# Hymba encoder block on one NeuronCore: the gate, scan and q/k/v stage as 64 slots in a written order

## The chip, the cores and the metric

One core of a Trainium2 chip runs the whole layer. A core has five engines with instruction queues of their own: PE (TensorE, matrix products), DVE (VectorE), ACT (ScalarE), POOL (GpSimd) and SP (SyncE, which only issues DMAs here). Each queue is executed strictly in order; an instruction that waits for a semaphore holds up all that stands behind it on its engine. ACT issues DMAs too, all the stores of the stage in question among them. The metric is the device time of one execution in microseconds (us), lower is better.

## The reference

Float32, T = 1024 tokens, D = 1024, one layer:

```python
h = rmsnorm(x, norm_mix_w)
z, xbc, dt_raw, q, k, v = split(h @ w_in)     # 1024 | 1536 | 32 | 1024 | 1024 | 1024 columns
xs, B, C = split(silu(conv5(xbc)))
# forward and backward chunked scan: 8 chunks of 128 tokens, 2 groups of 8 heads
seg    = a_cum[l] - a_cum[s]                   # per head, masked to l >= s
y_diag = (C B^T * exp(seg)) @ (xs*dt)          # inside a chunk
y_off  = (C @ state) * exp(a_cum)              # carried into a chunk
state  = decay * state + B^T @ (xs*dt*decay_to_end)
g   = (y_fwd + y_bwd + d_skip*xs) * silu(z);  y_ssm = rmsnorm per group(g)
q, k = rmsnorm per head(q), rmsnorm per head(k)
y_na = neighbourhood attention(q, k, v, rel_pos_bias)
x = x + concat(y_ssm, y_na) @ w_out
x = x + relu(rmsnorm(x) @ W1)^2 @ W2
```

Products are made in float32 accuracy from pairs of rounded operands: every factor is split into a high part (ACT, a copy that rounds) and a low part (DVE, a subtraction), and each product is three matmuls.

## The kernel before

The program runs in four stages: preparation and the xBC projection with the convolution (to about 172 us), the stage of this change (172 to 648 us), the attention with the output projection (to about 925 us), and the MLP. Tiles live in pools with a fixed number of buffers; a framework follows the data and puts in the semaphore waits, and a scheduler in it decides, from a model of costs, in which order each engine's instructions stand. The code only nudges it: `issue_after(mark)` forbids the work inside it to stand ahead of one instruction.

The stage computes 64 **pieces** `h[128 tokens] @ w[1024 x 512 columns]`: 16 for the gate z, then for each of two groups g 8 for q, 8 for k and 8 for v. A piece is 24 matmuls of 512 columns (8 steps along k, three products each, `mm3`, L181 to L183) into a PSUM bank. Its weights are four raw tiles of 128x1024, which `load_w` brings from HBM (L150) and splits into `wh` (ACT, L151) and `wl` (DVE, L152). There are two raw buffers for all stages and one more in this stage, so three here, and four pairs `wh`, `wl`.

After a piece:

- z: SiLU on ACT (L649), stored to `sz_dr` (L650).
- q and k (`normed`, `turned_split`): square on ACT (L330), sum per head on DVE (L332), the inverse root on POOL (`rq`, two instructions, L209 and L210), scaling on DVE (L334, from the same PSUM bank), four transposes on PE (L342, `ptq`), split into high on ACT (L194) and low on DVE (L195), and stored from ACT's queue: k by one DMA of 512 KB (L359), q by four of 128 KB (L352).
- v: split (L194, L195) and one store (L375).

Beside the pieces run, by `beside` and by the loop over `steps`:

- 14 **backward states** beside the first 18 pieces: an input loaded (L631), weighed on POOL (L416), split (L186, L187), one product `pS`, added on DVE (L617) and stored (L604).
- 32 **blocks** of decay differences: `seg_load` broadcasts two rows of `cum_dr` (`rb`, 512 KB, L391); POOL subtracts twice in place (L400); DVE selects by the mask in place (L406); ACT stores (L411). There are 4 buffers of `rb` beside the first pieces, and 1 in the later part.
- 16 **scan steps** (chunk c, group g): loads, `exp` of two blocks on ACT (L689), splits of `C`, the state and the weighed input (L186, L187), the product `pcb` (L705), D skip terms on DVE (L711, L715), `y` on POOL (L719), weighting by `pcb` on DVE (L721), state and carried products (`pS`, `py`), `yo` on DVE (L732) and its addition on POOL (L733), the inner product `pd` (L758), then addition of `pd` (L765), gate (L675), norm (ACT L677, POOL `ry` L209, L210), scaling and store of `y` (L679, L680).

Two PSUM banks named `tp` serve both the turned pieces and `pcb`. The attention then reads q, k and v back; a head pair's `q` is one DMA of 1 MB (L907).

Of the kernel before, what the change touches and what calls it, by code (L numbers as in the profile page):

```python
# [10 lines left out]
F32 = mybir.dt.float32  # L11
# [8 lines left out]
P = 128  # L20
# [36 lines left out]
def hymba_block(  # L57
# [35 lines left out]
    def enter_phase(ph, i, mm, extra):  # L93
        phase["ps"] = ph.enter_context(
            tc.tile_pool(name=f"ps{i}", bufs=1, space=PSUM, reuse_waits="tile")
        )
        phase["mm"] = mm
        phase["v"] = 4 - mm
        phase["w"] = [wp] * 3
        phase["r"] = [wp] * 2  # L100
        phase["n"] = 0
        if extra:
# [16 lines left out]
    q_dr = dr.tile([8, 4, HD, T], F32, name="q_dr")  # L119
# [4 lines left out]
    seg_dr = dr.tile([2, NT, P, 2, 512], F32, name="seg_dr")  # L124
    sb_dr = dr.tile([2, NT, P, 512], F32, name="sb_dr")
# [11 lines left out]
    def load_w(view, lo_eng, n=1024):  # L137
        pool = phase["w"][phase["n"] % len(phase["w"])]
        nb = phase["w"].count(pool)
        phase["n"] += 1  # L140
        rpool = phase["r"][phase["n"] % len(phase["r"])]
# [3 lines left out]
        hi = pool.tile([P, 1024], F32R, tag="wh", name="wh", bufs=nb)  # L145
        lo = pool.tile([P, 1024], F32R, tag="wl", name="wl", bufs=nb)
# [4 lines left out]
        nc.scalar.activation(hi[:, 0:n], raw[:, 0:n], AF.Copy)  # L151
        lo_eng.tensor_tensor(  # L152
            lo[:, 0:n], raw[:, 0:n], hi[:, 0:n].bitcast(F32), op=sub
        )
        return hi, lo

# [56 lines left out]
    with ExitStack() as ph:  # L213
# [98 lines left out]

        def hb(v):
# [5 lines left out]
        def qkv_proj(off, g):  # L319
            get = load_w_nat(w_in[0], 0, KD, off + 512 * g, nc.vector)  # L320
            for b in range(NT):
                pt = ps_mm("pq")
                for k in range(KD):
                    s = (slice(None), k, slice(b * P, (b + 1) * P))
                    mark = mm3(pt, hTh[s], hTl[s], *get(k), k == 0, k == KD - 1)
                yield b, pt, rcol[:, b : b + 1], mark.ins

        def normed(pt, rt):
            qn = hp.tile([P, 512], F32, tag="qn", name="qn", bufs=2)
            act = nc.scalar.activation(qn, pt, AF.Square, scale=rt)  # L330
            ss = hp.tile([P, 8], F32, tag="sq", name="sq", bufs=2)
            nc.vector.tensor_reduce(ss, h8(qn), axis=mybir.AxisListType.X, op=add)  # L332
            r = inv_rms(hp, ss, HD, 8, "rq")
            nc.vector.scalar_tensor_tensor(h8(qn), h8(pt), rt, hb(r), op0=mul, op1=mul)  # L334
            return qn, act.ins

        def turned_split(qn, w, mark):
            tp = ps_tp("ptq")
            with tc.issue_after(mark):
                for j in range(4):  # L340
                    s = slice(j * P, (j + 1) * P)
                    nc.tensor.transpose(tp[:, s], qn[:, s], ident)  # L342
            hl = hp.tile([P, 2, 512], F32R, tag="hl", name="hl", bufs=2)
            split_from_psum(hl[:, 0], hl[:, 1], tp, w)
            return hl.bitcast(F32).rearrange("f a (p t) -> f a p t", p=4)

        def store_q(g, b, qn, mark):
            hl = turned_split(qn, pcol[:, 80:81], mark)
            s = slice(b * P, (b + 1) * P)
            for j in range(2):  # L350
                for a in range(2):
                    nc.scalar.dma_start(  # L352
                        q_dr[4 * g : 4 * g + 4, 2 * j + (a ^ j), :, s].rearrange("p d t -> d p t"),
                        hl[j * HD : (j + 1) * HD, a],
                    )

        def store_k(g, b, qn, mark):
            hl = turned_split(qn, pcol[:, 81:82], mark)
            nc.scalar.dma_start(  # L359
                k_dr[g, :, :, :, b * P : (b + 1) * P].rearrange("a p f t -> f (a p) t"),  # L360
                hl.rearrange("f a p t -> f (a p) t"),
            )

        def qkv_units():
            held = None
            for g in range(2):
                for off in (OFF_Q, OFF_K, OFF_V):
                    for b, pt, rt, mark in qkv_proj(off, g):
                        if held is not None:
                            held(mark)  # L370
                            held = None
                        if off == OFF_V:
                            hl = hp.tile([P, 8, 2, HD], F32R, tag="hl", name="hl", bufs=2)
                            split_from_psum(hl[:, :, 0], hl[:, :, 1], h8(pt), rt)
                            nc.scalar.dma_start(v_dr[b, :, 8 * g : 8 * g + 8], hl.bitcast(F32))  # L375
                            act = None
                        else:
# [1097 lines left out]
```

## Time and profile before

| what | value |
|---|---|
| time, median of 3 runs | 1655.78 us (1651.81 to 1657.99) |
| the profiled execution's own time | 1659.05 us |
| its span | 1657.3 us (1.75 us of its time lie outside) |
| granted TensorE clock, mean over the span | 0.982 |
| DMA issues of the stage: q stores / block stores / k stores | 64 / 32 / 16 |

The columns of a window row are: the window, its length, then for PE, PEld (weight loads), DVE, ACT and POOL the busy time with the count of instructions in brackets, the granted TensorE clock, the share of DMA time and GB/s. A row of waits names engine, line and tile that waited, then what ended the wait, the total in us, how many there were, and the longest. A row of groups has line, engine, operation, tiles and shapes, count, busy us and the mean of one in ns, and the idle time before it with what ended it. In a timeline, an `[idle before <-releaser]` at the end of a row gives the stall ahead of it.

### The profile page before, as it was taken

Reading aid. Unit: us, or ns where it says so; the run is one execution under the profiler, and the core shown is the slowest. Engines: PE = TensorE matmul, PEld = TensorE weight load, DVE = VectorE, ACT = ScalarE, POOL = GpSimd, SP = SyncE. Lnnn points to the kernel's source line nnn. Section 1 sums busy time; section 2 is a strip of 40 time slices with the busy share of each in tenths; the row PEclk is TensorE's granted clock in tenths of the full one; section 3 lists DMA queues with packets and bytes.
Section 4 is the critical chain, followed back from the end, with each engine's and each line's share of the span. In section 5 each row is a group of like instructions: output and inputs, shape, how many; then the busy total and the mean of one; then the engine's idle time right before and its main releaser. Section 6 shows DMA issues by size and latency. Waiting matters only on the chain. (4 is left out here: it accounts for less than half of the span.)

```text
span 1657.3 us, 20925 instructions
## 1 busy us (share of the span) xinstructions
PE 1589.3 (96%) x7462; PEld 1300.0 (78%) x7462; DVE 1017.6 (61%) x1420; ACT 719.1 (43%) x1183; POOL 714.6 (43%) x520
## 2 busy tenths in 40 slices
PE   7999988998989999999998998999999989999999
PEld 6788867877867888887887776888888868888887
DVE  4777455477657773666665477434244388887863
ACT  5434322254334344566675334444444534433330
POOL 3000266467546744232353332344444555455551
PEclk9999999999999999999999998999999989999999
DMA  8113688897877669968772430453444486644332
GB/s 207 53 38 102 194 266 260 222 304 212 271 210 191 190 196 308 270 171 206 207 218 77 131 123 26 151 180 117 146 157 140 163 295 214 216 142 150 102 102 77
DMA packets 190243, 290.28 MB, mean 175 GB/s; under 512 B 15715, under 2 KB 106939, under 8 KB 190139
## 3 DMA queue, kind: packets, MB, share of 16 engines
q1 hardware_dynamic: 141547, 239.65, 47.4%
q10 hardware_dynamic: 47584, 45.62, 8.5%
q0 software_dynamic: 1008, 3.67, 0.5%
q8 instruction: 59, 0.97, 0.2%
q14 instruction: 45, 0.37, 0.1%
HBM read 197.27 MB, written 94.95 MB: 176 GB/s over the span
## 5 line engine op out<-in xcount | busy, mean ns | idle before, releaser
L187 POOL TENSOR_TENSOR wl<-wraw,wh 128x1024 fp32r<-128x1024 f32 x110 | 298.3, 2722 | 320.0 <-ACT wh L186 305.5
L186 ACT ACTIVATE wh<-wraw 128x1024 fp32r<-128x1024 f32 x110 | 115.5, 1054 | 150.1 <-PE px L804 50.7
L804 PE MATMUL px<-wh,ahl 128*128 128x512 f32 x512 | 162.4, 395 | 3.3 <-ACT ahl L186 3.3
L182 PE MATMUL pq<-wl,hTh 128*128 128x512 f32 x384 | 152.9, 399 | 6.7 <-DVE wl L152 6.7
L181 PE MATMUL pq<-wh,hTh 128*128 128x512 f32 x384 | 152.1, 401 | 7.0 <-ACT wh L151 5.3
L804 PE MATMUL px<-h,wh 128*128 128x512 f32 x496 | 156.0, 396 | 1.6 <-DVE x L1156 1.6
L183 PE MATMUL pq<-wh,hTl 128*128 128x512 f32 x384 | 152.4, 398 | 0.0
L187 DVE TENSOR_TENSOR ahl<-ar,ahl 128x1024 fp32r<-128x1024 f32 x56 | 114.7, 2055 | 23.3 <-ACT ahl L186 22.2
L186 ACT ACTIVATE ahl<-ar 128x1024 fp32r<-128x1024 f32 x56 | 58.2, 1052 | 140.0 <-PE px L804 76.4
L804 PEld LDWEIGHTS px<-wh,ahl 128*128 128x128 f32 x512 | 97.1, 190 | 25.0 <-ACT ahl L186 3.7
L804 PEld LDWEIGHTS px<-h,wh 128*128 128x128 f32 x496 | 93.2, 188 | 24.2 <-ACT h L191 1.8
L804 PE MATMUL px<-wl,ahl 128*128 128x512 f32 x256 | 100.9, 395 | 0.0
L400 POOL TENSOR_TENSOR rb<-rb,c 128x512 f32<-128x512 f32 x64 | 71.2, 1134 | 67.6 <-DMA rb<-cum_dr 57.0
L804 PE MATMUL px<-h,wl 128*128 128x512 f32 x248 | 98.1, 395 | 0.0
L182 PEld LDWEIGHTS pq<-wl,hTh 128*128 128x128 f32 x384 | 73.4, 191 | 22.9 <-DVE wl L152 8.4
L181 PEld LDWEIGHTS pq<-wh,hTh 128*128 128x128 f32 x384 | 73.2, 191 | 22.8 <-ACT wh L151 6.6
L151 ACT ACTIVATE wh<-wraw 128x1024 fp32r<-128x1024 f32 x58 | 60.6, 1057 | 66.8 <-DMA wraw<-in_w_in_dram 30.3
L191 ACT ACTIVATE pth<-ptp 128x384 fp32r<-128x384 f32 (+1 forms) x128 | 56.9, 457 | 66.0 <-PE ptp L1014 65.5
L183 PEld LDWEIGHTS pq<-wh,hTl 128*128 128x128 f32 x384 | 73.3, 191 | 15.0
L804 PE MATMUL pz<-h,wh 128*128 128x512 f32 x256 | 82.2, 402 | 0.4 <-DVE h L192 0.4
L804 PE MATMUL pz<-wh,ahl 128*128 128x512 f32 x256 | 80.5, 391 | 0.0
L181 PE MATMUL po<-wh,yh 128*128 128x512 f32 x192 | 76.5, 398 | 2.1 <-DVE x L888 1.8
(273 smaller groups left out, 4031.9 us busy)
## 6 DMA issues: line engine op xcount, KB each, us to landing
ar<-act_dr SPq DMA_DIRECT2D x56, 512.0 KB, 3.6
act_dr<-cq SPq DMA_DIRECT2D x49, 512.0 KB, 3.0
wraw<-in_w_in_dram SPq DMA_DIRECT2D x44, 512.0 KB, 4.3
rb<-cum_dr SPq DMA_DIRECT2D x32, 512.0 KB, 6.6
wraw<-in_w_mlp_in_dram SPq DMA_DIRECT2D x32, 512.0 KB, 4.7
wraw<-in_w_mlp_out_dram SPq DMA_DIRECT2D x32, 512.0 KB, 4.3
seg_dr<-rb ACTq DMA_DIRECT2D x32, 256.0 KB, 2.9
q_dr<-hl ACTq DMA_DIRECT2D x64, 128.0 KB, 3.8
```

The source lines that it names most:

```text
L151: nc.scalar.activation(hi[:, 0:n], raw[:, 0:n], AF.Copy)
L181: nc.tensor.matmul(pt, lhsT=ah, rhs=bh, start=first, stop=False)
L182: nc.tensor.matmul(pt, lhsT=ah, rhs=bl, start=False, stop=False)
L183: return nc.tensor.matmul(pt, lhsT=al, rhs=bh, start=False, stop=last)
L186: nc.scalar.activation(hl[0], src, AF.Copy)
L187: eng.tensor_tensor(hl[1], src, hl[0].bitcast(F32), op=sub)
L191: top = nc.scalar.activation(hi, src, AF.Copy)
L400: nc.gpsimd.tensor_tensor(rb[:, d], rb[:, d], c1[:, d, c, h0 : h0 + 4].unsqueeze(2).broadcast_to([P, 4, P]), op=sub,)
L804: nc.tensor.matmul(pt, lhsT=a, rhs=b, start=f, stop=l, skip_group_check=True)
```

## The change

The stage is written anew as a loop over 68 slots. `slot(k)` holds piece k and, in the order in which its lines stand, everything else that is done beside it. All instructions a slot issues, on every engine, are chained to the one before on the same engine (`in_order`), SP's and ACT's DMA issues too; so the scheduler has no choice left in slots 0 to 67. What is computed stays the same, and so does the number of PE's instructions.

- **Order of pieces**: z, z, then q, v, k for each group (before: q, k, v).
- **Delays**: piece k's square or split stands in slot k+1, its transposes in the middle of piece k+2, the split of the turned piece in slot k+3. A list `late` collects the transposes and the scan's products; they are issued in the middle of the next piece, after four of its eight k steps. A list `stores` collects the stores of a slot; they are issued on ACT's queue in the next slot, ahead of the work of that slot.
- **Scan steps** begin at the slots in `starts`, and spread over five slots; **blocks** are loaded at the slots in `seg_at`, subtracted and selected two slots later. The difference goes into a tile of its own, `seg` (3 buffers, later 2), and the second half stays in `rb` (3 buffers, later 2).
- **Weights**: a fourth raw buffer; all four raw loads of the next column set are issued in a set's second slot, two tiles are split in the middle of its last slot, one at the end of it, and the fourth ahead of the next set's first piece.
- **q** is laid out in DRAM like k: one store of 512 KB per piece, and four loads in place of one per head pair later. `seg_dr` and `sb_dr` become one DRAM tile per step. The loads and stores that build the bias table are spread over slots 24 to 51.

```diff
-        phase["r"] += [wx]
+        phase["r"] += [wx] * 2
...
-    q_dr = dr.tile([8, 4, HD, T], F32, name="q_dr")
+    q_dr = dr.tile([2, 2, 4, P, T], F32, name="q_dr")
...
+        cols += [off + 512 * g for g in range(2) for off in (OFF_Q, OFF_V, OFF_K)]
...
+        def piece(k):
+            j, b = divmod(k, 8)
+            pt = out_pt[k] = ps_mm("pz" if j < 2 else "pq")
+            for i in range(KD):
+                if i == 4:
+                    while late:
+                        late.pop(0)()
+                hi, lo = tiles[j][i // 2]
...
+                mm3(pt, hTh[s], hTl[s], hi[:, w], lo[:, w], i == 0, i == KD - 1)
...
+        def seg_select(n):
+            g, c, q = seg_of(n)
+            rb, seg = rbs.pop(n)
+            nc.vector.copy_predicated(
+                seg, lmask.unsqueeze(1).broadcast_to([P, 4, P]), rb[:, 1]
+            )
+            stores.append(
+                partial(nc.scalar.dma_start, seg_dr[c, g][:, q], seg.rearrange("p h s -> p (h s)"))
+            )
...
+        starts = (20, 22, 25, 27, 30, 32, 35, 38, 40, 42, 44, 47, 50, 52, 55, 57)
...
+        def slot(k):
+            j, b = divmod(k, 8)
+            if k < 64:
+                if b == 0 and j:
+                    w_splits(j, 1)
+                piece(k)
+            else:
+                while late:
+                    late.pop(0)()
+
+            if b == 1 and j < 7:
+                raw_loads(j + 1)
...
+            for f in [stores.pop(0) for _ in range(len(stores))]:
+                f()
...
+            leave(k - 1)
+            split_turned(k - 3)
+            for a in at(k, 5):
+                put_y(*a)
+            for a in at(k, 4):
+                gate(*a)
+            for a in at(k, 2):
+                diagonal(*a)
...
+            scale(k - 1)
+            for a in at(k, 4):
+                norm(*a)
+            if b == 7 and j < 7:
+                w_splits(j + 1, 2)
+            for a in at(k, 2):
+                decayed(*a)
+            if seg is not None:
+                seg_subtract(seg)
...
+            if seg is not None:
+                seg_select(seg)
+
+            for a in at(k, 0):
+                late.append(partial(products, *a))
...
+            if b == 7 and j < 7:
+                w_splits(j + 1, 1)
...
+            with in_order():
+                slot(k)
...
-            nc.sync.dma_start(q.bitcast(F32), q_dr[p].rearrange("(h a) d t -> (a d) h t", h=2))
+            for j in range(2):
+                for a in range(2):
+                    nc.sync.dma_start(
+                        q[a * HD : (a + 1) * HD, j].bitcast(F32),
+                        q_dr[p // 4, a ^ j, p % 4, j * HD : (j + 1) * HD],
+                    )
```

In the changed kernel's own lines the square is L590, the sum L592, the scaling L598, the transposes L604, the split L201 and L202, the subtraction L651, the selection L662, all stores of a slot L854 and the matmuls of a piece L188 to L190.

Where it moves instructions, at three places.

**ACT, the store of a block.** Before, in the second half of the stage (`hl` is a split piece, `wh` a weight tile, `chl`, `shl` and `xhl` operands of the scan):

```order
L680 DMA y_dr<-y_3132 128x512
L194 ACTIVATE hl<-ptq,pcol 128x512
L151 ACTIVATE wh<-wraw 128x1024
L411 DMA seg_dr<-rb 128x512
L359 DMA k_dr<-hl 128x8x128
L186 ACTIVATE chl<-cT 128x128
L186 ACTIVATE shl<-st 128x512
L194 ACTIVATE hl<-ptq,pcol 128x512
```

and in the changed kernel, two slots of the first k set:

```order
L854 DMA k_dr<-hl 128x8x128
L854 DMA seg_dr_82<-seg 128x512
L590 ACTIVATE qn<-pq,rcol 128x512
L201 ACTIVATE hl<-ptq,pcol 128x512
L825 ACTIVATE y_3461<-y_3461,ry 128x512
L826 DMA y_dr<-y_3461 128x512
L854 DMA k_dr<-hl 128x8x128
L590 ACTIVATE qn<-pq,rcol 128x512
```

The stores of the slot before, the block's among them, now stand directly ahead of the square of the last piece; before, a square stood wherever the scheduler had put it, here not next to the block's store at all.

**DVE, one slot's list.** Before, in the second group's part of the stage (`sq` the sum per head, `qn` the scaled piece, `rb` the block selected):

```order
L195 SCALAR_TENSOR_TENSOR hl<-pq,rcol,hl 128x8x64
L406 COPY_PREDICATED rb<-lmask,rb 128x512
L187 TENSOR_TENSOR chl<-cT,chl 128x128
L152 TENSOR_TENSOR wl<-wraw,wh 128x1024
L332 TENSOR_REDUCE sq<-qn 128x8
L765 TENSOR_TENSOR y_3812<-y_3812,pd 128x512
L675 TENSOR_TENSOR y_3812<-y_3812,sz 128x512
L406 COPY_PREDICATED rb<-lmask,rb 128x512
L743 COPY st<-pS 128x512
L332 TENSOR_REDUCE sq<-qn 128x8
```

and in the changed kernel slot 44, in which one step begins, one is in its third slot and one in its fifth:

```order
L770 TENSOR_TENSOR st<-st,pS 128x512
L780 TENSOR_TENSOR yo<-py,e_132 128x512
L592 TENSOR_REDUCE sq<-qn 128x8
L202 SCALAR_TENSOR_TENSOR hl<-ptq,pcol,hl 128x512
L815 TENSOR_TENSOR y_4068<-y_4068,pd 128x512
L816 TENSOR_TENSOR y_4068<-y_4068,sz 128x512
L787 SCALAR_TENSOR_TENSOR pcb,cd<-pcb,ident 128x128
L789 SCALAR_TENSOR_TENSOR cf<-dt,cd,dsk 128x8
L598 SCALAR_TENSOR_TENSOR qn<-pq,rcol,rq 128x512
L796 TENSOR_TENSOR gm<-gm,pcb 128x512 x2
L194 TENSOR_TENSOR xl<-xw,xh 128x512
L662 COPY_PREDICATED seg<-lmask,rb 128x512
```

The selection, which stood between other work, is now the last of its slot's list, and the sum per head stands near the front of it.

**PE, the end of the stage.** Before (`psc` the attention's first scores, `pty` and `po` the output projection's first pieces):

```order
L181 MATMUL pq<-wh,hTh 128x512
L182 MATMUL pq<-wl,hTh 128x512
L183 MATMUL pq<-wh,hTl 128x512
L985 MATMUL psc<-k,q 128x256
L988 MATMUL psc<-kl,q 128x256
L985 MATMUL psc<-k,q 128x384
L988 MATMUL psc<-kl,q 128x384
L862 MATMUL pty<-ident,yl 128x128 x8
```

and in the changed kernel:

```order
L188 MATMUL pq<-wh,hTh 128x512
L189 MATMUL pq<-wl,hTh 128x512
L190 MATMUL pq<-wh,hTl 128x512
L1146 MATMUL psc<-k,q 128x384
L1149 MATMUL psc<-kl,q 128x384
L604 MATMUL ptq<-ident,qn 128x128 x8
L1018 MATMUL pty<-ident,yl 128x128 x4
L188 MATMUL po<-wh,yh 128x512
```

The last pieces are now of k and not of v, so the transposes of the last two stand behind the last piece, between the attention's first scores and the output projection.

More of the change, by code (lines that the diff above doesn't have):

```diff
@@ L1 @@
-from contextlib import ExitStack
+from contextlib import ExitStack, contextmanager
 from functools import partial
@@ L311, in hymba_block @@
         nc.sync.dma_start(dsk, d_skip.partition_broadcast(P)[:, 0, :])
-        def hb(v):
-            return v.unsqueeze(2).broadcast_to([P, 8, HD])
-        def h8(v):
-            return v.rearrange("p (e d) -> p e d", d=HD)
[L319 to L377, printed above, removed]
-                            qn, act = normed(pt, rt)
-                            held = partial(store_q if off == OFF_Q else store_k, g, b, qn)
-                        yield mark, act
@@ L652, in hymba_block @@
-            units = qkv_units()
-            for n in range(16, 21):
-                beside(n, *next(units))
-        with ExitStack() as p2:
-            qp = p2.enter_context(tc.tile_pool(name="qs", bufs=2, side="right", reuse_waits="tile"))
-            zt = qp.tile([P, 192], F32, tag="y1", name="zt")
-            nc.gpsimd.memset(zt, 0.0)
-            for r0 in (0, 23):
+        zp = p1.enter_context(tc.tile_pool(name="zp", bufs=2, side="right", reuse_waits="tile"))
+        p2 = ExitStack()
@@ new lines, in scale, with turn @@
+        def scale(k):
+            if k in turning:
+                qn, r, pt, rt = turning[k]
+                nc.vector.scalar_tensor_tensor(h8(qn), h8(pt), rt, hb(r), op0=mul, op1=mul)
+                def turn():
+                    tp = ps_tp("ptq")
+                    for i in range(4):
+                        s = slice(i * P, (i + 1) * P)
+                        nc.tensor.transpose(tp[:, s], qn[:, s], ident)
+                    turning[k].append(tp)
+                late.append(turn)
@@ new lines, in back_add @@
+        def back_add(m, new):
+            c, g = back[m]
+            if g in blast:
+                nc.vector.tensor_tensor(new, new, bpS.pop(m), op=add)
+            else:
+                nc.vector.tensor_copy(new, bpS.pop(m))
+            blast[g] = new
+            stores.append(partial(nc.scalar.dma_start, sb_dr[c - 1, g], new))
+        starts = (20, 22, 25, 27, 30, 32, 35, 38, 40, 42, 44, 47, 50, 52, 55, 57)
+        begin = {k: n for n, k in enumerate(starts)}
+        X = {n: {} for n in range(16)}
@@ new lines, in hymba_block, with at, loads @@
+        st, ahead = {}, {}
+        def at(k, off):
+            n = begin.get(k - off)
+            return [] if n is None else [(n, *steps[n], X[n])]
+        def loads(n, c, g, v):
+            v["xs"] = t512("xs", 2)
+            nc.sync.dma_start(v["xs"], xs_dr[c, :, g * 512 : (g + 1) * 512])
+            v["gm"] = []
+            for q in range(2):
+                gm = pool["p"].tile([P, 4, P], F32, tag=f"gm{q}", name="gm", bufs=2)
+                nc.sync.dma_start(gm.rearrange("p h s -> p (h s)"), seg_dr[c, g][:, q])
+                v["gm"].append(gm)
```

547 lines of the change are left out of this document (321 added, 226 removed).

## The prediction

> **What bounds the kernel now.** I read the page first, then the stage by windows, then who waits for whom, then single costs.
>
> ```profile
> span 1657.3 us, 20925 instructions
> PE 1589.3 (96%) x7462; PEld 1300.0 (78%) x7462; DVE 1017.6 (61%) x1420; ACT 719.1 (43%) x1183; POOL 714.6 (43%) x520
> ```
>
> PE sets the time. The change touches the stage from 171.8 to 648.3 us. Its windows (length, then busy time of PE, PEld, DVE, ACT, POOL, the clock, DMA):
>
> ```profile
> 171.80:648.30 476.50, 450.15 (x2138) 371.06 (x2137) 293.28 (x417) 173.82 (x285) 274.62 (x261) 0.98 0.78 234
> 302.00:601.00 299.00, 281.96 (x1401) 233.74 (x1400) 210.32 (x325) 125.08 (x215) 189.31 (x181) 0.99 0.76 225
> 601.00:648.30 47.30, 47.30 (x230) 39.69 (x229) 16.91 (x31) 14.11 (x23) 12.97 (x15) 1.00 0.88 266
> ```
>
> PE idles 476.50 - 450.15 = 26.35 us in the stage. From 302 to 601 us, where 38 pieces end together with the scan, it is busy 281.96/38 = 7.42 us per piece, DVE 5.53, POOL 4.98, ACT 3.29. No engine is full beside PE. In the last 47 us PE never idles. Four stretches run at half clock, 20.4 us together (the first and the last are shown), and cost half of that, 10.2 us:
>
> ```profile
> 233.70:240.50 6.80, 6.12 (x15) 4.70 (x15) 3.27 (x5) 1.32 (x2) 4.36 (x4) 0.50 0.74 231
> 493.10:496.50 3.40, 2.87 (x10) 2.61 (x11) 2.57 (x5) 1.14 (x3) 3.15 (x5) 0.50 0.34 83
> ```
>
> So before pays 26.35 + 10.2 = 36.5 us over its bare matmuls. A rewritten order can win at most that; an idle us has cost 36.5/26.35 = 1.39 us, with the clock. What PE waits for in the stage is mainly weights and the scaled piece:
>
> ```profile
> PE pq L182 <- DVE wl L152: 6.7, 4, 4.9
> PE ptq L342 <- DVE qn L334: 6.4, 3, 3.4
> PE pq L181 <- ACT wh L151: 5.3, 3, 2.7
> PE pz L181 <- ACT wh L151: 2.3, 1, 2.3
> ```
>
> **The change, part by part.** The weights first. At the second column set of the gate the timeline shows
>
> ```profile
> 226.56 0.50 PE L182 MATMUL pz<-wl,hTh 128*128 128x512 f32 x1 [1.41 <-DVE wl L152]
> 232.16 0.74 PE L181 MATMUL pz<-wh,hTh 128*128 128x512 f32 x2 [2.32 <-ACT wh L151]
> 234.53 0.79 PE L182 MATMUL pz<-wl,hTh 128*128 128x512 f32 x1 [0.68 <-DVE wl L152]
> ```
>
> With four raw buffers and loads six slots ahead, no raw tile is late there. These stalls, 4.4 us, and the 3.4 us of half clock behind them should go. I remove all of before's 36.5 us and count the new order's losses from zero.
>
> The new order's bare slot: a piece is 24 matmuls of 512 columns, by this row of the chain of waits 24 x 10.89/48 = 5.45 us.
>
> ```profile
> 1368.69 10.89 PE px L804 x48
> ```
>
> Transposes and the scan's products come on top: slot 43, for one, has 5.45 + 0.40 (four transposes) + 0.12 (`pcb`) + 6 x 0.23 + 8 x 0.22 (inner products; these small ones are my estimates, a half to one 512-column matmul each) = 9.1 us; slot 42, with transposes alone, 5.85. Slots 20 to 52 come to 234 us, 7.1 each.
>
> The other engines now run each slot as one list, and the lists hold each other by a loop. ACT issues the block's store of slot k-1 ahead of the square in slot k; that store waits for the selection, the last of DVE's list in slot k-1. Behind it stand, one after another: square, sum per head (DVE), inverse root (POOL), in some slots `y` work on POOL, two subtractions (POOL), the selection (DVE), the next store. Their prices:
>
> ```profile
> L406 DVE COPY_PREDICATED rb<-lmask,rb 128x512 f32<-128x512 int32 x32 | 39.6, 1239 | 54.2 <-POOL rb L400 49.2 <-DMA sz_dr<-zs 3.7 <-DMA wraw<-in_w_in_dram 1.3
> L334 DVE SCALAR_TENSOR_TENSOR qn<-pq,rcol,rq 128x512 f32<-128x512 f32 x32 | 24.0, 749 | 28.0 <-POOL rq L210 28.0
> L195 DVE SCALAR_TENSOR_TENSOR hl<-ptq,pcol,hl 128x512 fp32r<-128x512 f32 x32 | 23.8, 743 | 7.8 <-ACT hl L194 7.1 <-DMA gm<-seg_dr 0.7
> L332 DVE TENSOR_REDUCE sq<-qn 128x8 f32<-128x512 f32 x32 | 21.6, 677 | 4.7 <-ACT qn L330 4.6
> L675 DVE TENSOR_TENSOR y<-y,sz 128x512 f32<-128x512 f32 x16 | 12.2, 762 | 1.7 <-DMA sz<-sz_dr 1.5
> L765 DVE TENSOR_TENSOR y<-y,pd 128x512 f32<-128x512 f32 x16 | 10.9, 681 | 3.0 <-PE pd L758 2.1 <-POOL y L733 0.9
> L330 ACT ACTIVATE qn<-pq,rcol 128x512 f32<-128x512 f32 x32 | 21.7, 681 | 37.1 <-PE pq L183 25.8 <-DMA q_dr<-hl 5.6 <-PE pd L758 3.0
> L677 ACT ACTIVATE sz<-y 128x512 f32<-128x512 f32 x16 | 10.0, 626 | 22.3 <-DVE y L675 14.2 <-DMA q_dr<-hl 5.4 <-DVE pcb L711 2.8
> L400 POOL TENSOR_TENSOR rb<-rb,c 128x512 f32<-128x512 f32 x64 | 71.2, 1134 | 67.6 <-DMA rb<-cum_dr 57.0 <-DVE yo L732 4.4 <-DMA sz_dr<-zs 4.3
> L210 POOL TENSOR_TENSOR rq<-rq,half 128x8 f32<-128x8 f32 x32 | 55.1, 1723 | 2.2
> L733 POOL TENSOR_TENSOR y<-y,yo 128x512 f32<-128x512 f32 x28 | 38.8, 1386 | 15.1 <-DVE yo L732 13.7
> L719 POOL TENSOR_TENSOR y<-xs,cf 128x512 f32<-128x512 f32 x16 | 17.1, 1071 | 19.8 <-DVE cf L715 16.5 <-ACT gm L689 3.1
> L209 POOL TENSOR_SCALAR rq<-sq 128x8 f32<-128x8 f32 x32 | 13.4, 420 | 29.4 <-DVE sq L332 27.8
> L210 POOL TENSOR_TENSOR ry<-ry,half 128x1 f32<-128x1 f32 x16 | 11.1, 694 | 1.0
> L209 POOL TENSOR_SCALAR ry<-ss 128x1 f32<-128x1 f32 x16 | 5.9, 367 | 15.1 <-ACT sz L677 14.1
> 304.37 0.44 ACTq L411 DMA_DIRECT2D seg_dr<-rb  x1
> 304.91 2.69 ACTq L352 DMA_DIRECT2D q_dr<-hl  x4
> ```
>
> The two `rq` rows give the root: 0.42 + 1.72 = 2.14 us; the two `ry` rows give 1.06. A turn of the loop is then 0.44 + 0.68 + 0.68 + 2.14 + 2 x 1.13 + 1.24 = 7.45 us; with `y` (1.07) and one addition (1.39) on POOL 9.9 us. Where a step is in its fifth slot, the path by split, gate and norm is 0.44 + 0.68 + 0.68 + 0.74 + 0.68 + 0.76 + 0.63 + 1.06 + 2.26 + 1.24 = 9.2 us. Some 0.06 us for each hand-over is added by estimate, 0.3 to 0.7 us a turn. In the 22 slots of 20 to 52 that select a block, the longest path of each comes to 7.1 to 10.3 us, 9.1 on average: 2 us over PE's 7.1, or 44 us. In the 11 others DVE's list alone counts (2 to 9.3 us) and the lag shrinks again.
>
> How much lag PE bears: the transposes of a piece stand in the middle of the piece after the next, 1.5 slots or about 9 us after its end, and need square, sum, root and scaling first, 0.68 + 0.68 + 2.14 + 0.75 = 4.25 us; the rest is about 5 us. The `pcb` products bear less, since they need a `tp` bank that the split frees: near 3 us. In slots 42 and 43 the loop takes 10.3 and 4.0 us where PE takes 5.8 and 9.1: a lag of 4.5 us, and none left behind it. In slots 26 to 32, where every slot selects, it takes 9.9, 8.2, 7.1, 9.1, 7.1, 9.1 and 8.2 us against 6.9, 6.1, 8.7, 6.1, 7.2, 6.9 and 6.1: it gains 10.7 us on PE. Running so through the slots, with lag never under zero and all beyond the bound charged to PE, I get 22 us of stalls at 5.7 us and 29 at 3; I take 25.5, most of it in slots 26 to 36, 39, 40 and 48 to 52.
>
> Before shows that such waits are real though nobody strings them together:
>
> ```profile
> DVE rb L406 <- POOL rb L400: 49.2, 24, 6.8
> POOL rq L209 <- DVE sq L332: 27.8, 13, 3.4
> DVE hl L195 <- ACT hl L194: 31.1, 15, 4.8
> DVE xhl L187 <- ACT xhl L186: 21.5, 7, 15.8
> ```
>
> There the order lets something else run past them on PE's behalf. The last two waits, 52.6 us together, recur inside DVE's lists (the high part on ACT comes just ahead of each low part). Nothing of them on PE's path is one bound, half the other; I take a quarter, 13 us.
>
> Further new losses. Weight splits: three of four tiles of a set (DVE 1.35 us each) go into the last slot of the set before, where DVE's list then has 7 to 10 us against PE's 6 to 9.1; what the loop has not yet counted I put at 5 us (0 to 10). The first backward product moved to slot 3 waits for its load, weighing and split: 3 us (0 to 6). At the end, k is last and not v: behind the last piece PE has four short score products and then the last pieces' transposes, which need the 4.25 us above: 4 us (0 to 5). The window from 601 us, without idle time, shows that before pays nothing there.
>
> What costs nothing: the q stores, 48 fewer issues of 2.69/4 = 0.67 us each on ACT, which is busy 3.3 of 7.4 us; their waits are in the 36.5 already. The q loads, 24 more in the attention:
>
> ```profile
> q<-q_dr SPq DMA_DIRECT2D x1, 1024.0 KB, 8.5
> ```
>
> A pair's q lands in 8.5 us and is prefetched by a pair; without that cover it would be 8.5 us once. The bias table's transfers stand in SP's queue ahead of the scan's loads; those are issued a slot or more ahead, and one late transfer would be some us. The own tile `seg` takes away the wait for `rb`'s buffer; it doesn't shorten the loop.
>
> Sum: idle time 25.5 + 13 + 5 + 3 + 4 = 50.5 us, with the clock 50.5 x 1.39 = 70 us, less 36.5: +34 us. On the profiled execution's 1659.05 that is 1693, which stood 3.3 us over the median: **1690 us**.
>
> One rule speaks on the factor 1.39. The Trainium skill, "TensorE: Matmul & The Clock Gate", section "Why this matters for your kernels", asks for no idle gaps of PE over some 3 us, since one idle window brings the clock back to half. By it most of my stalls, 1 to 4 us each, would cost no clock, and the sum would be 50.5 - 36.5, some 1670 us. The trace disagrees so far: the three gaps of 1.41, 2.32 and 0.68 us quoted above were followed by 6.8 us at half clock.
>
> **The rivals.**
>
> Covered lists, faster: the lag never passes PE's slack, since PE's slots vary and 11 of 33 have no block. For it: DVE's 5.53 us per piece and POOL's 4.98 leave a quarter of the time free. Against it: the loop is a sum of waits on four engines, not a load of one. Then about 10 us idle stay (end, first product, a hand-over), 14 with the clock: 1655.8 - 22.5 = 1633 us.
>
> Balance, the same: the loop costs half of what I think and DVE's waits little, 26 us idle like before: 1656 us. That the change doesn't act at all is excluded as far as the order rows go; I put it in here.
>
> Full chain, slower still: DVE's waits count half (26), the loop 29, the weights 10, and 6 and 5 elsewhere: 76 us idle, 106 with the clock, less 36.5: 1725 us. It takes over where DVE idles in most slots for the square; for it speaks the 49.2 us in 24 waits, 2 us each.
>
> **How the numbers follow.** Forecast case 0.50, full chain 0.22, balance 0.10, covered lists 0.18. What lies within 0.5% (1647.5 to 1664 us) can't be told from no change here. Faster 0.18, same 0.10, slower 0.72. The range 1638 to 1728 holds the forecast's own range (1669 with 36 us idle: loop 22, waits 6, the rest 8; 1705 with 62: 29, 20, 13), and leaves out half of the covered lists and the end of the full chain.
>
> **What would show it.** Right: in slots 20 to 52 the square waits for a block's store, whose releaser is the selection on DVE, and PE's waits there are for the scaled piece or the `tp` split; more PE idle time than 26.35 us in the stage, in the two groups' q and v sets; the gate's second set without a stall for weights; a gap of about 4 us ahead of the last transposes. Wrong: PE busy over 95% from slot 20 to 52; or a long wait for DMA (`gm`, `rb`) in the place of the loop; or idle time as forecast at full clock, which would make the rule above right.

## The result, and the profile after

The changed kernel takes 1709.15 us (median of 4 runs, 1706.46 to 1711.72) against 1656.19 us before (4 runs): ratio 1.0324, 95% interval 1.0298 to 1.035. It is 53 us slower; 34 were forecast.

The page of the changed kernel, profiled execution:

```profile
span 1704.7 us, 20838 instructions
PE 1600.6 (94%) x7462; PEld 1307.9 (77%) x7462; DVE 1017.6 (60%) x1420; ACT 716.7 (42%) x1183; POOL 697.9 (41%) x520
```

No engine has more instructions to do than before. PE is busy 11 us longer with the same 7462 matmuls, for the greater part because more of them ran at half clock; POOL is busy 17 us less. Almost all of the 47.4 us of longer span is time in which PE waits or runs at half clock. The windows after (first the 17 pieces up to the end of the first q piece, then the other 47 pieces, all 64, and the start of the attention):

```profile
174.40:283.20 108.80, 107.02 (x468) 87.27 (x467) 50.13 (x52) 32.42 (x45) 52.38 (x46) 0.98 0.72 231
283.20:687.30 404.10, 355.38 (x1666) 292.77 (x1665) 238.11 (x362) 136.04 (x237) 204.16 (x212) 0.94 0.67 211
174.40:687.30 512.90, 462.39 (x2132) 380.03 (x2131) 288.24 (x413) 168.46 (x282) 256.54 (x258) 0.95 0.68 215
687.30:740.00 52.70, 42.42 (x230) 35.75 (x229) 29.75 (x71) 26.79 (x65) 17.34 (x18) 0.87 0.99 273
```

and the same pieces before:

```profile
172.00:290.90 118.90, 109.59 (x462) 88.31 (x461) 61.60 (x57) 33.24 (x45) 66.80 (x59) 0.94 0.78 242
290.90:648.60 357.70, 340.66 (x1678) 282.84 (x1677) 231.68 (x360) 140.56 (x240) 208.13 (x202) 0.99 0.78 231
648.60:700.00 51.40, 50.67 (x287) 42.55 (x285) 34.18 (x86) 32.53 (x80) 20.47 (x18) 1.00 1.02 278
```

The first 17 pieces became 10.1 us faster, the other 47 became 46.4 us slower, what follows 8.7 us slower, and the stage starts 2.3 us later: 47.4 in all. PE idles 50.5 us in the stage and 10.3 us behind it. The half clock takes nine stretches of the stage in place of four, 51.2 us together, and 13.7 us more behind it; two of them are shown below. What such a stretch costs is half of the time in which PE is busy in it, since the rest is idle time and already counted. PE is busy in 40.6 of the 51.2 us and in 5.6 of the 13.7, and before in 16.9 of 20.4. So the half clock costs 20.3 and 2.8 us, against 8.4 before.

```profile
509.40:516.20 6.80, 3.81 (x12) 3.23 (x13) 3.35 (x6) 3.12 (x6) 2.88 (x3) 0.50 0.21 77
690.30:704.00 13.70, 5.65 (x21) 4.68 (x22) 3.98 (x7) 3.81 (x5) 8.82 (x9) 0.50 0.86 261
```

What PE waits for in slots 17 to 63, and behind them:

```profile
PE pcb L744 <- DVE hl L202: 20.2, 7, 5.8
PE ptq L604 <- DVE hl L202: 11.6, 4, 6.1
PE py L188 <- DVE st L770: 6.0, 2, 3.6
PE pq L189 <- DVE wl L194: 5.0, 3, 1.9
...
PE ptq L604 <- DVE qn L598: 9.4, 1, 9.4
```

Before, PE waited for weights and for the scaled piece. Now 31.8 us are waits for the split `hl`, which frees a `tp` bank for the next transposes or for `pcb`. The last row is the end, behind the last piece.

**The loop, in slots 42 and 43 of the changed kernel**, read against the clock (timeline; start, duration):

```profile
505.94 0.52 POOL L216 TENSOR_SCALAR ry<-ss 128x1 f32<-128x1 f32 x1
507.06 1.04 POOL L651 TENSOR_TENSOR seg<-rb,c 128x512 f32<-128x512 f32 x1
508.06 1.04 POOL L651 TENSOR_TENSOR rb<-rb,c 128x512 f32<-128x512 f32 x1
...
509.13 0.73 DVE L662 COPY_PREDICATED seg<-lmask,rb 128x512 f32<-128x512 int32 x1 [2.73 <-POOL rb L651]
...
509.89 0.34 ACTq L854 DMA_DIRECT2D seg_dr<-seg  x1
510.27 0.69 ACT L590 ACTIVATE qn<-pq,rcol 128x512 f32<-128x512 f32 x1 [5.07 <-DVE seg L662]
510.86 0.68 ACT L201 ACTIVATE hl<-ptq,pcol 128x512 fp32r<-128x512 f32 x1
...
511.60 0.74 DVE L202 SCALAR_TENSOR_TENSOR hl<-ptq,pcol,hl 128x512 fp32r<-128x512 f32 x1
...
512.39 0.80 PE L744 MATMUL pcb<-cT,bT 128*128 128x128 f32 x2 [5.81 <-DVE hl L202]
```

The root of the norm, two subtractions, selection, store, square, the two halves of the split, `pcb`: each begins as the one before it ends, on four engines, and PE stands for 5.81 us at the end of it. (The root here is that of `y`, and its second half ends at 507.09.)

**The end.** The last piece is done at 687.3; its root is the second POOL row and the last:

```profile
685.55 4.70 POOL L194 TENSOR_TENSOR wl<-wraw,wh 128x1024 fp32r<-128x1024 f32 x2 [0.81 <-ACT wh L193]
690.33 0.20 POOL L216 TENSOR_SCALAR rq<-sq 128x8 f32<-128x8 f32 x1
692.67 2.37 POOL L1097 TENSOR_TENSOR mb<-braw,nam 128x384 f32<-128x384 f32 x3 [2.14 <-DMA braw<-t_dr]
694.99 1.65 POOL L217 TENSOR_TENSOR rq<-rq,half 128x8 f32<-128x8 f32 x1
...
697.57 1.09 PE L604 MATMUL ptq<-ident,qn 128*128 128x128 f32 x4 [9.45 <-DVE qn L598]
```

The output projection's weight split (4.70 us) stands ahead of the root, and the attention's bias work, which itself waits for a transfer, between the root's two halves. The edges chain the slots' instructions to each other, not what the scheduler puts between them.

### The profile page after: what moved, and what is told of

Same layout as the page of the kernel before. It is cut to its first block, busy times and chain, and to the rows that moved or that the text cites. A ratio compares the mean times of both kernels' runs of the same rounds, so it can differ in the third digit from the quotient of the medians.

```text
span 1704.7 us, 20838 instructions
## 1 busy us (share of the span) xinstructions
PE 1600.6 (94%) x7462; PEld 1307.9 (77%) x7462; DVE 1017.6 (60%) x1420; ACT 716.7 (42%) x1183; POOL 697.9 (41%) x520
## 5 line engine op out<-in xcount | busy, mean ns | idle before, releaser
L194 POOL TENSOR_TENSOR wl<-wraw,wh 128x1024 fp32r<-128x1024 f32 x128 | 341.1, 2676 | 367.6 <-ACT wh L193 353.2
L188 PE MATMUL pq<-wh,hTh 128*128 128x512 f32 x384 | 155.8, 406 | 2.8 <-ACT wh L193 2.8
L190 PE MATMUL pq<-wh,hTl 128*128 128x512 f32 x384 | 152.7, 398 | 0.0
L188 PEld LDWEIGHTS pq<-wh,hTh 128*128 128x128 f32 x384 | 74.6, 194 | 19.1 <-ACT wh L193 3.8
L190 PEld LDWEIGHTS pq<-wh,hTl 128*128 128x128 f32 x384 | 74.0, 193 | 16.2
L188 PE MATMUL po<-wh,yh 128*128 128x512 f32 x192 | 77.2, 402 | 2.6 <-ACT yh L1000 1.0
L1164 ACT ACTIVATE pr<-pr,nmx 128x384 f32<-128x384 f32 (+1 forms) x128 | 74.9, 586 | 7.6 <-DVE nmx L1154 5.5
L1097 POOL TENSOR_TENSOR mb<-braw,nam 128x256 f32<-128x256 f32 (+1 forms) x48 | 38.4, 828 | 96.7 <-DVE nmx L1154 62.8
```

Of the source, the lines that this page charges most:

```text
L188: nc.tensor.matmul(pt, lhsT=ah, rhs=bh, start=first, stop=False)
L190: return nc.tensor.matmul(pt, lhsT=al, rhs=bh, start=False, stop=last)
L194: eng.tensor_tensor(hl[1], src, hl[0].bitcast(F32), op=sub)
L1097: nc.gpsimd.tensor_tensor(mb[:, s].rearrange("p (s r c) -> p s r c", r=16, c=8), v[:, a:b], nam[:, s].rearrange("p (s r c) -> p s r c", r= ...
L1164: nc.scalar.activation(pr[:, 0:n], pr[:, 0:n], AF.Exp, bias=nmx[:, b : b + 1], scale=-1.0, accum_out=db,)
```

## The experiments

To compare kernels with the same order on PE, I take for each slot the time from its piece's first matmul to the next piece's, less the shortest seen in any of the eight kernels with that order. The sums of this excess, in us with the half clock in it, for slots 0 to 16, for the slots around a change of column set (23, 24, 31 to 33, 39 to 41, 47 to 49), and for the other slots. A wait that all eight kernels share is not in these sums.

| kernel | 0 to 16 | change of set | the others |
|---|---|---|---|
| the change | 1.6 | 33.9 | 28.0 |
| the end changed (slots as in the change) | 1.8 | 35.3 | 32.2 |
| store behind the square | 1.7 | 29.4 | 28.4 |
| subtractions first | 7.2 | 30.7 | 1.5 |
| and fourth split behind | 6.6 | 23.6 | 5.9 |
| and raw loads spread | 1.8 | 25.2 | 3.1 |
| the change, raw loads spread | 1.7 | 28.5 | 40.0 |
| subtractions first, no low weights | 7.6 | 9.3 | 10.4 |

The second row tells by how much one profile differs from the next with the same slots: about 5 us.

### No edges

```diff
-            with in_order():
-                slot(k)
+            slot(k)
```

> The edges that hold every engine's order are left out; the order in which the work is written, the buffers, the layout of q and the order of pieces stay, and the scheduler puts the instructions in order by its own model, as before. If the fixed order is the cause, the time goes back to that of before or a little under it, 1640 to 1665 us. If piece order, delays and buffers are the cause, it stays at 1690 or over.

1656.76 us, ratio 0.9991 (0.9973 to 1.0008). The fixed order is the cause; the order of the pieces, the delays and the layout of q cost nothing in a free order. From slot 27 to the last piece PE has only two waits over 0.4 us, 0.81 and 0.91. What is left stands mainly in two places, the second of them the end, as in the change:

```profile
356.18 1.09 PE L604 MATMUL ptq<-ident,qn 128*128 128x128 f32 x4 [6.87 <-ACT hl L201]
647.17 1.09 PE L604 MATMUL ptq<-ident,qn 128*128 128x128 f32 x4 [10.07 <-DVE qn L598]
```

### Store behind the square

```diff
             leave(k - 1)
             split_turned(k - 3)
+            for f in [seg_stores.pop(0) for _ in range(len(seg_stores))]:
+                f()
```

(`seg_select` appends to `seg_stores` in place of `stores`.)

> Only the block's store moves on ACT's queue, from ahead of the square to behind the square and the split of the same slot; DVE's and POOL's lists stay. Loop theory: a turn of the loop loses the store (0.34 us), the square (0.69) and a hand-over, some 1.2 of 9 us; DVE still runs the selection ahead of the next sum. The running sum of chain less PE work falls by about half, 12 us of idle time, 18 with the clock: 1691 us (1683 to 1700). Rival A, the store is no part of it and DVE's list alone holds PE up: 1705 to 1713. Rival B, late transfers: the same, 1705 to 1713.

1705.11 us, 1.0293 (1.0268 to 1.0319), not to be told from the change. The store is at most a small link. In slot 43 the wait shown above falls from 5.81 to 3.96 us, and PE's waits of `pcb` for the split from 20.2 to 14.8 us together, but slot 27 grows by 3.7 us and the time doesn't tell the sum from nothing. DVE still runs the selection ahead of the next sum and the next split, so the loop closes on DVE's queue without ACT. My reading of the link was wrong, and rival A names the right engine.

### Subtractions first

```diff
+            if seg is not None:
+                seg_subtract(seg)
             if m in bxs:
...
             split_turned(k - 3)
+            if seg is not None:
+                seg_select(seg)
...
-            if seg is not None:
-                seg_subtract(seg)
...
-            if seg is not None:
-                seg_select(seg)
```

> The two subtractions move to the front of POOL's list of the slot, the selection on DVE to just behind the split of the turned piece. Loop theory: the store then follows a selection that is long done, and no turn leads through root, y work and subtraction; PE's waits for the tp banks and the scaled piece (38 us in slots 18 to 63) fall to some 15 us, with the clock 35 us less: 1674 us (1662 to 1690); what stays is the end of the stage (17 us with its clock) and the weight tiles. Rival A, the sum of work per slot on DVE is the bound: 1700 to 1712. Rival C, the root now waits behind 2.1 us of subtractions and the scaled piece is late instead: 1705 or more.

1683.53 us, 1.0158 (1.0132 to 1.0184): 1.66% or 27 us off the change, with the same instructions and no work left out. The excess of the other slots falls from 28.0 to 1.5 us; that of the changes of set stays. So the loop is shown, by its POOL and DVE links together (the two moves were not run apart), and cutting it is worth 27 us with the clock. The rival that the root would be late falls: in the stage PE never waits for the scaled piece. There is one new cost. In slot 4 the subtractions now wait 7.61 us for their block's load, the weighing of a backward input stands behind them on POOL, and PE waits 3.71 us for it; this, with the half clock behind it, is the 7.2 us in the table's first column. What stays is, in slots 47 and 48 of this kernel:

```profile
533.82 3.62 DVE L194 TENSOR_TENSOR wl<-wraw,wh 128x1024 fp32r<-128x1024 f32 x2
540.21 2.34 DVE L194 TENSOR_TENSOR wl<-wraw,wh 128x1024 fp32r<-128x1024 f32 x2
543.08 0.73 DVE L202 SCALAR_TENSOR_TENSOR hl<-ptq,pcol,hl 128x512 fp32r<-128x512 f32 x1
...
534.32 2.03 POOL L651 TENSOR_TENSOR seg<-rb,c 128x512 f32<-128x512 f32 x1
...
543.96 0.77 PE L744 MATMUL pcb<-cT,bT 128*128 128x128 f32 x2 [4.39 <-DVE hl L202]
```

Four low splits of weights, 5.96 us of DVE, stand ahead of the split that PE waits for.

### Fourth split behind

```diff
                 if b == 0 and j:
+                    for f in [stores.pop(0) for _ in range(len(stores))]:
+                        f()
+                    leave(k - 1)
+                    split_turned(k - 3)
                     w_splits(j, 1)
```

(on top of the subtractions first; these calls are then skipped further down in such a slot)

> On top of the kernel with the subtractions first: in the first slot of a column set the square or split of the piece before and the split of the turned piece stand ahead of the fourth weight tile's split, on ACT and on DVE. In the kernel with the subtractions first, slots 23/24, 31/32, 40/41 and 48/49 are 41 us longer than their bare matmuls. Theory: the tile's 1.05 us on ACT and 1.2 to 1.8 on DVE, behind three others, make the split late that frees the tp bank; with them behind it, half of the 41 us goes: 1664 us (1655 to 1674). Rival: DVE's list over the two slots is longer than PE's work in any order, the stall moves to the weights of the next piece: 1678 to 1688.

1681.33 us, 1.0132 (1.01 to 1.0164), not to be told from the kernel it stands on. Excess went from the first slot of a set to the second: slot 48 came from 6.8 to 1.2 us, slot 49 from 4.4 to 8.3. By the time this is the rival's outcome: another order only moves the lag. But the rival's reason, lists on DVE longer than PE's work, is not what slot 49 shows. There PE waits 9.34 us for the split `hl`, DVE idles 5.79 us just ahead of its half of that split, and ACT's half waits for the store of q:

```profile
556.17 0.69 ACT L201 ACTIVATE hl<-ptq,pcol 128x512 fp32r<-128x512 f32 x1 [6.17 <-DMA q_dr<-hl]
```

### No low weights

```diff
-                tiles[j].append(split_raw(raws[j].pop(0), nc.vector))
+                nc.scalar.activation(hi, raws[j].pop(0), AF.Copy)
+                tiles[j].append((hi, hi))
```

(for all column sets but the first, on top of the subtractions first; the kernel leaves the low parts of the weights out of its result, and PE multiplies by the high part in their place, so it has as many matmuls)

> The kernel with the subtractions first (1683.5), without the low parts of the weights in all column sets but the first: DVE's 28 subtractions of 1.2 to 1.8 us are left out, and PE multiplies by the high part a second time in the low part's place, so its work and its times stay; the result lacks the low parts. If DVE's list at the change of sets holds the split that frees the tp bank, the 41 us over bare matmuls in slots 23/24, 31/32, 40/41 and 48/49 fall to some 12: 1654 us (1645 to 1664). If the late stores of splits and ACT's own weight copies do it, most stays: 1672 to 1684.

1673.29 us, 1.0106 (1.0087 to 1.0125): 0.5% or 9 us less than the kernel it stands on; by the time alone that is the rival's range. By slots it is a mixture: the excess at the changes of set falls from 30.7 to 9.3 us, while slots 26 and 36 take 8 us more, with waits for an operand (2.60 us) and for the `tp` bank (2.29 us) that the kernel with the low splits did not have there. So about two thirds of the excess at the changes of set come from DVE's low splits, though only 9 us of it come out as time; 8.7 of the 9.3 us left are slot 49 alone:

```profile
537.18 0.38 ACTq L861 DMA_DIRECT2D q_dr<-hl  x1
538.49 0.34 ACTq L861 DMA_DIRECT2D seg_dr<-seg  x1
538.93 0.69 ACT L201 ACTIVATE hl<-pq,rcol 128x512 fp32r<-128x512 f32 x1 [5.40 <-DMA wraw<-in_w_in_dram]
546.08 0.69 ACT L201 ACTIVATE hl<-ptq,pcol 128x512 fp32r<-128x512 f32 x1 [6.46 <-DMA q_dr<-hl]
...
547.70 1.08 PE L611 MATMUL ptq<-ident,qn 128*128 128x128 f32 x4 [9.50 <-DVE hl L202]
```

There are two `hl` tiles, and a tile is free when its store has landed. At the passage from q to v, ACT's split waits 6.46 us for the store of q, beside the raw loads. What ended the wait of 5.40 us is the landing of a weight tile that the waiting instruction doesn't read. It stands behind two stores on ACT's queue, and those wait for such landings: in the trace each of the two carries the semaphore of a raw load, issued at 529.69 and 530.25, and is issued as that load has landed (the second store at 538.49, its load at 538.47). So a load can hold up a store that has nothing to do with it, and with it all of ACT's queue.

### Raw loads spread

```diff
-            if b == 1 and j < 7:
-                raw_loads(j + 1)
+            if 1 <= b <= 4 and j < 7 and k < 64:
+                raw_loads(j + 1, (b - 1,))
```

> The changed kernel, with the four raw weight loads of the next column set issued one each in the second to fifth slot of a set in place of all four in the second. Theory (rival B at the set boundaries): in slot 48/49 ACT's split waits 6.44 us for the store of an earlier split, which shares the DMA engines with 2 MB of raw loads, and PE then 6.05 us for the tp bank; spread, those waits shrink, here and near slot 33 and 41: some 10 us of idle time in all, with the clock 15: 1694 us (1688 to 1702). Rival: the store is late because of its place on ACT's queue and not because of the loads: 1705 to 1712.

1712.24 us, 1.0333 (1.031 to 1.0356): no gain. In the change, slot 49 shows the store's landing beside four raw loads:

```profile
565.45 3.36 SPq L148 DMA_DIRECT2D wraw<-in_w_in_dram  x4
...
571.69 0.38 ACTq L854 DMA_DIRECT2D q_dr<-hl  x1
583.12 0.69 ACT L201 ACTIVATE hl<-ptq,pcol 128x512 fp32r<-128x512 f32 x1 [6.44 <-DMA q_dr<-hl]
```

With the loads spread, the same places read:

```profile
580.49 0.38 ACTq L854 DMA_DIRECT2D q_dr<-hl  x1
587.37 0.69 ACT L201 ACTIVATE hl<-ptq,pcol 128x512 fp32r<-128x512 f32 x1 [0.52 <-DMA q_dr<-hl]
...
588.99 0.63 PE L604 MATMUL ptq<-ident,qn 128*128 128x128 f32 x4 [2.44 <-DVE hl L202]
...
369.29 0.69 ACT L201 ACTIVATE hl<-pq,rcol 128x512 fp32r<-128x512 f32 x1 [7.24 <-DMA v_dr<-hl]
```

The expected wait fell from 6.44 to 0.52 us, and PE's from 6.05 to 2.44. But in slot 28 a v split now waits 7.24 us for a v store that meets a later raw load, and that slot became 6.7 us longer. This fits loads that make stores late, where spreading them evenly only chooses other stores: beside four raw loads the q store above took 11.4 us to land, while the one issued at 548.37 took 3.42. But the store of 571.69 was also issued late. Its semaphore was that of a block's load issued at 565.04, which landed at 571.61. No run separates what the late issue cost from what the landing cost.

> The spread raw loads on top of the kernel with the subtractions first and the fourth split behind. If loads crowd the stores, the 9.34 us wait of slot 49 and most of the rest at the boundaries go: 1664 us (1656 to 1672). If ACT's place of the store is it, 1676 to 1684.

On top of the fourth split behind: 1673.73 us, 1.0097 (1.0077 to 1.0117), against 1.0132 (1.01 to 1.0164). The intervals touch; by the medians of the ratios it is 6 us, most of it in slot 4 (4.8 us of excess less). Slot 49 keeps its wait (8.37 us), so the cause that was expected at the changes of set isn't the one that acted.

### v last in the second group

```diff
-        cols += [off + 512 * g for g in range(2) for off in (OFF_Q, OFF_V, OFF_K)]
+        cols += [off + 512 * g for g in range(2) for off in ((OFF_Q, OFF_V, OFF_K), (OFF_Q, OFF_K, OFF_V))[g]]
```

> In the second group the order of pieces becomes q, k, v, as before the change; the first group stays q, v, k. Nothing has to be turned behind the last piece. Theory: the 9.45 and 0.78 us of waiting at the end and the 13.7 us at half clock behind it go, 17 us; slots 48 to 55 become k pieces beside the same scan steps, which costs up to 8 us by the loop: 1696 us (1690 to 1706). Rival: the end waits for transfers and weights of the attention anyway, the gap only moves: 1705 to 1712.

1707.5 us, 1.0309 (1.0279 to 1.0339): a miss. The 9.45 us wait is gone, but the same place now waits for the output projection's weights. Slot 49, where no q meets a v any more, is 7.7 us shorter (6.6 in place of 14.3); slots 51, 52, 53 and 56, now with k pieces, are 10.7 us longer together (slot 52 takes 10.7 us in place of 6.2):

```profile
698.73 1.06 ACT L193 ACTIVATE wh<-wraw 128x1024 fp32r<-128x1024 f32 x1 [4.71 <-DMA wraw<-in_w_out_dram]
...
700.41 0.79 PE L188 MATMUL po<-wh,yh 128*128 128x512 f32 x1 [4.71 <-ACT yh L201]
```

### The end changed

```diff
+                with after_root():
+                    mb = bias_for(2 * p + hh)
...
+                    eng = nc.gpsimd if part + h else nc.vector
+                    get = load_w_nat(w_out[0], 512 * part, 4, 512 * h, eng)
```

(`after_root` chains the POOL instructions made in it behind the last inverse root.)

> The changed kernel with its slots as they are; only POOL's queue at the end: the attention's bias work stays behind the last inverse root, and the first weight tiles of the output projection are split on DVE in place of POOL. Theory: the 9.45 us gap is the last root waiting behind POOL's weight split (4.7 us) and, between its two halves, bias work that waits for a transfer; without them the gap is the chain of 4.3 us: 5 us of idle time and 3 to 7 us of half clock less, 1699 us (1694 to 1704). Rival: the gap is the price of turning a piece at the end at all: 1707 to 1712.

1706.36 us, 1.0289 (1.0256 to 1.0322); the medians differ by less than the intervals. The gap itself is shorter:

```profile
696.50 1.09 PE L608 MATMUL ptq<-ident,qn 128*128 128x128 f32 x4 [4.01 <-DVE qn L602]
699.68 1.11 PE L1022 MATMUL pty<-ident,yl 128*128 128x128 f32 x4 [2.10 <-DVE hl L202]
```

9.45 us became 4.01, the bare chain of root and scaling, so POOL's queue was the cause of the rest. But 2.10 us came in behind it (a split waits 4.5 us for a k store), and the half clock stayed at 13.7 us. Net some 3 us in the profile.

> The kernel without the edges, with the same change at the end. There the gap is 10.1 us with 13.7 us of half clock behind it. Theory as for the run above, some 10 us off 1656.8: 1646 us (1641 to 1652), under the kernel before. Rival: 1655 to 1659.

On top of no edges: 1651.35 us, 0.9959 (0.9941 to 0.9977), faster than before by 0.4%. The gap came from 10.07 to 4.54 us and the half clock from 13.7 to 10.2 us.

> The spread raw loads on top of the kernel without edges and with the end changed (1651.4). There one piece takes 15.9 us, with a 7.05 us wait for a split on ACT. If loads crowd the stores there too, 8 to 10 us less: 1643 us (1637 to 1648). If not, or if the scheduler finds another order, 1649 to 1656.

1651.27 us, 0.9961 (0.9947 to 0.9975): the spread loads change nothing in the free order either; the piece of 15.9 us takes 16.5. These two are the only kernels here that beat the one before.

### Two parts of the change on the kernel before

```diff
-            phase["r"] += [wx]
+            phase["r"] += [wx] * 2
...
+            nc.scalar.dma_start(
+                q_dr[g, :, :, :, b * P : (b + 1) * P].rearrange("a p f t -> f (a p) t"),
+                hl.rearrange("f a p t -> f (a p) t"),
+            )
```

> The kernel before, its scheduler and its order of pieces, with two parts of the change alone: the fourth raw buffer, and q laid out like k (one store of 512 KB per piece, four loads per head pair). Theory: the gate's stalls for weights (4.4 us, with 3.4 of half clock) go, and ACT's 48 issues of 0.67 us fewer take some waits for the scaled piece away: 1643 us (1635 to 1652). Rival: the scheduler finds another order that pays elsewhere: 1652 to 1662.

1675.86 us, 1.0109 (1.0078 to 1.0139): slower, a miss. With two parts that were to take waits away, the scheduler found another order. Of PE's three longest waits there, the second and third are new; the first is 5.62 us where before had 4.90 us at the same hand-over:

```profile
283.99 0.79 PE L182 MATMUL pq<-wl,hTh 128*128 128x512 f32 x1 [5.62 <-DVE wl L152]
403.25 1.09 PE L342 MATMUL ptq<-ident,qn 128*128 128x128 f32 x4 [5.45 <-DVE qn L334]
487.44 0.80 PE L181 MATMUL pq<-wh,hTh 128*128 128x512 f32 x1 [6.65 <-ACT wh L151]
```

So the fourth buffer did not spare this hand-over of weights. The two parts were not run apart, so which of them moved the order is open.

## Why the prediction was right, and where its sizes were off

The sign was right, the loop is real, and 1709 us lies in the range. But the loop is 27 of the 84 us that PE now loses, the largest loss stood at the changes of set, and 1709 is about as far from the 1690 of the forecast as from the 1725 of the full chain. The terms of the sum, with their clock factor, against what the slots show:

| step | forecast, idle and with 1.39 | measured, with the clock |
|---|---|---|
| before's losses, taken away | 36.5 | 35.5, replaced by 84 |
| loop | 25.5, 35 | 27 |
| waits inside DVE's lists | 13, 18 | not seen apart from the loop and the sets |
| weight splits at the change of set | 5, 7 | 34 |
| first backward product | 3, 4 | 3.9 (slot 3 takes 10.1, slot 4 with such a product too 6.2) |
| end | 4, 6 | 13 (10.3 idle, 2.8 clock) |

That the sum came within 20 us is in part luck. The loop and the waits in DVE's lists were put at 53 us together, and the slots from 17 on that lie away from a change of set hold 28 us of excess; the weight splits and the end were put at 13 and came to 47. Two errors of opposite sign nearly cancelled.

1. *No raw tile late at the gate's second set*: right, no stall for weights there; slots 0 to 16 are 10.1 us shorter.

2. *The loop of store, square, sum, root, subtraction, selection*: right as a loop, by the run with the subtractions first (27 us). PE waits for the split that frees a `tp` bank, as was named; the scaled piece, named beside it, makes up only 1.2 us in the stage. The places were partly others: slots 32 and 36, in the first k set and not in a q or v set, hold 15.6 of the 63.5 us of excess. Two steps of the loop failed. The store's place on ACT is not what closes it (the run with the store behind); the selection on DVE ahead of the next sum is enough. And the prices were means over instructions that run alone and beside the other engine: 1.24 us for a selection that takes 0.73 alone, 1.13 for a subtraction that takes 1.04.

3. *What the loop has not yet counted I put at 5 us*: the step that failed most. The changes of set cost 34 us; without DVE's low splits 21 of 31 us of excess go, in the kernel with the loop cut. I had counted DVE's list against PE's work over one slot and left out that the split freeing the `tp` bank stands behind all four weight splits, and that a 512 KB store holds one of two `hl` tiles until it has landed. That also goes against a part of *what costs nothing*: one q store of 512 KB is fewer issues, but its landing, 11.4 us by 571.69 to 583.12 in slot 49, is on the path. (The 8.5 us for a q load was the shortest of three that can be read in the profile of before; the others took 13.8 and 15.0.)

4. *The last pieces' transposes, 4 us*: the chain was right (4.01 us in the run with the end changed), but POOL's other work stood inside it, because edges between slots hold nothing that isn't in a slot.

5. *An idle us costs 1.39 us*: 60.8 us idle and 23.1 us lost at half clock make it 1.38, so the factor held. The prediction's own sum for before was too high, since half of each whole stretch (10.2 us) counts the idle time inside the stretches once more; by PE's busy time it is 8.4 us, and the factor of the stage before 1.32. The new losses less the old, 83.9 - 35.5 = 48.4 us, come near the 45.0 us that the stage and what follows became longer.

6. The Trainium skill, "TensorE: Matmul & The Clock Gate", section "Why this matters for your kernels", warns of gaps of more than some 3 us. The trace agrees for these: all six (3.49, 3.57, 3.77, 5.81, 6.05, 9.45 us) ended in a stretch at half clock or began one. But shorter gaps are not safe: of the ten from 1.5 to 3 us five did as well (2.23 and two of 1.56 did; 2.52, 2.75 and another of 1.56 didn't). The sum that follows from the rule alone, 1670, was further off than the one from the rows.

Of the rivals, covered lists and balance fall. Full chain, 1725 us, had the right direction for the size. Its sign came about: DVE idles for the square 23 times in 47 slots (40.8 us, longest 6.1). But what was missing in the forecast came from the changes of set and the end, and not from the loop and DVE's waits, where this rival had put it.

## What to carry to other kernels

When an order is written out by hand, look for the ring: the last instruction of one engine's list that another engine needs first in the next round. Moving the two subtractions and the selection behind them to the front of their lists took 27 us away; moving the issue of a store between them changed the time by no more than its scatter. Count the work at the seams (change of weights, end of the stage) against what stands in front of the one instruction that frees a bank, and remember that instructions outside the chained part still share the queues. A free scheduler that overlaps the same work at 0.9991 is the bound to beat before an order is fixed.

## What the runs showed of the hardware that was not expected

DVE and POOL can slow each other when both work in SBUF at once. In the changed kernel a selection takes 0.73 us when POOL is idle (509.13 above), and 1.56 beside POOL's work, which here takes no longer than its usual 1.04:

```profile
554.23 1.04 POOL L676 TENSOR_TENSOR xw<-xs,wd 128x512 f32<-128x512 f32 x1
...
554.30 1.56 DVE L662 COPY_PREDICATED seg<-lmask,rb 128x512 f32<-128x512 int32 x1 [3.60 <-POOL rb L651]
```

There is little in between: of the 32 selections 16 take 0.71 to 0.76 us, among them all 14 beside an idle POOL, and the 16 that overlap POOL's work by about 1 us or more take 1.55 to 1.59. In the kernel with the subtractions first, a subtraction takes 2.03 us and two low splits 3.62 us where they overlap (534.32 and 533.82 above), against 1.04 and 2.34 apart. The Trainium skill, "GPSIMD Engine Reference", section "8. Key points", says that the two share their SBUF interfaces and contend when DVE has two SBUF inputs; the trace agrees, and adds the factor of up to two.

Around the gap of 9.45 us the clock stood at half for 13.7 us, four times the 3.4 us of the shortest such stretch. It fell 2.2 us after PE's last matmul, while PE idled, and stayed at half for 6.4 us after PE had work again at 697.57. Shortening the gap to 4.01 and 2.10 us left those 13.7 us as they were.
